# Moving the block sums of a seven-product down-projection in SBUF, and ordering its products by operand

## The chip, the cores and the metric

The kernel runs on one core of a Trainium2 chip. The metric is the device time of one execution in microseconds. Times are medians over several runs; the profile is of one further execution.

## What is computed

The reference is a decoder trunk with 256 tokens (S), width 1024 (D_MODEL) and two layers, in float32. Layer 0 mixes tokens by dilated attention, layer 1 by forgetting attention; behind each stands a SwiGLU feed-forward of inner width 2816 (D_FF). The change touches the feed-forward alone:

```python
def swiglu(h, w_gu, w_down):
    gu = h @ w_gu
    g, u = gu[..., :D_FF], gu[..., D_FF:]
    return (jax.nn.silu(g) * u) @ w_down
```

## The kernel before, in words

**Split products.** Every large operand is kept as a pair of tiles: a high part (ScalarE, L80) and a low part, the rest (VectorE, L84). The names end in `h` and `l`: `wh`, `wl` for weights, `ah`, `al` for activations, `sh`, `sl` and `th`, `tl` for the sums below. A product of two such pairs is three matmuls, high by high (L239), then stationary high by moving low and stationary low by moving high (L244). This is `mm3`; its second argument is the stationary operand, its third the moving one. In the trace, the moving operand comes first: `ps_tr<-th,sh` has `th` moving and `sh` stationary.

**The feed-forward** (`ffn`, from L741). The 22 feature tiles f are worked in order. `up(f)` multiplies the normed activations `xt` (moving) by a tile of gate and up weights (stationary), 48 matmuls of 128x256, forms silu(g)·u, and splits it into half of an activation tile `a`. Two feature tiles make one step j of the down-projection (11 steps). After the up-projection of an even f, the step j = f/2 − 1 is done: `down(j, 0)` and `down(j, 1)` are the first 512 output columns for the two token halves (128x512 matmuls, `a` stationary, the weights moving), and for j < LATE = 9 `down_7(j)` does the other 512 columns for both halves. For these, two token halves, two feature tiles and two column blocks of 256 form a 2x2 block product, which `down_7` does with seven products in place of eight, as Strassen's scheme does. Steps 9 and 10 do it with plain `down` products.

**The seven products.** They are named by their sums: p1, p6, c11, c12, c21, q5, q7; each is 3 matmuls of 128x256, so a call is 21 matmuls, and there are 9 calls a layer. p1 and c11 multiply plain activations `a` by plain weights `w`; c21 multiplies `a` by a block sum of weights, `t`; c12 and q5 multiply a block sum of activations, `s`, by `w`; p6 and q7 multiply `s` by `t`. `combine` (L752) makes `s` on VectorE and allocates it under the tag "v" (7 buffers); `sums_of` (L119) makes `t` and allocates it under the tag "bias" (4 buffers). The accumulators stand in four PSUM tiles: c11 and c12 in one of `acc[0]` (`ps_sc` in the trace), c21 in one of `acc[1]` (`ps_o`), p1 with p6 and q5 with q7 in two more (`ps_tr`). They accumulate over the nine calls; `gather` (L777) then adds p1, p6, q5 and q7 into the residual rows, for token half 0 right after the last call, in a chain of steps on ScalarE (L786) and VectorE (L787 to L795). `residual` (L693) adds the remaining sums.

**What orders the work.** The program is written in the order in which TensorE takes it; the other engines' instructions are placed by a scheduler, with `first()` raising the urgency of some. Weights are loaded on SP's queue and split ahead by `weights`, which runs two tiles ahead of the use; their tiles `wh` and `wl` are rings of four.

**Addresses.** Tiles of one partition row are laid out one behind the other, so the size of a tile sets the address of all that is allocated behind it. In the program before, the starts modulo 128 bytes are: `wh` and `wl` 96, `xt` 32, `ah` and `al` 96, `sh` and `sl` 96, `th` and `tl` 0.

Of the kernel before, what the change touches and what calls it, by code (L numbers as in the profile page):

```python
# [11 lines left out]
F32R = mybir.dt.float32r  # L12
# [5 lines left out]
P = 128  # L18
D = 1024
S = 256  # L20
# [12 lines left out]
def trunk(ctx: ExitStack, tc: tile.TileContext, T, out):  # L33
# [4 lines left out]
    ap = ctx.enter_context(tc.tile_pool(name="ap", bufs=1))  # L38
# [5 lines left out]
    def first():  # L44

        return tc.high_priority(offset=300)

    def psum(tag):
        return ps.tile([P, 512], F32, tag=tag, name=f"ps_{tag}", bufs=2)
# [26 lines left out]
    def split(pair, view, src, early=True, after=None, hold=None):  # L76
        hi, lo = pair
        with first() if early else nullcontext():
            with behind_(hold):
                a = nc.scalar.activation(view(hi), src, AF.Copy)  # L80

            def low(after=None):
                with tc.issue_after(after.ins) if after else nullcontext():
                    return nc.vector.tensor_tensor(view(lo), src, view(hi).bitcast(F32), op=ALU.subtract)  # L84

            if isinstance(after, list):
                return after.append(low)
            return a, low(after)
# [30 lines left out]
    def sums_of(key, w):  # L119

        if key[1] == LATE - 1:
            raw = [wp.tile([P, 1024], F32, tag="raw", name="raw", bufs=5) for _ in range(2)]
        else:
            both_f = ap.tile([P, KT * S], F32, tag=("oth", "otl")[key[1] % 2], name="rawd", bufs=1)
            raw = [both_f[:, c * 1024:(c + 1) * 1024] for c in range(2)]
        for c in range(2):
            nc.sync.dma_start(raw[c], T[key[0]][key[1]][:, c * 1024:(c + 1) * 1024])
        b11, b12, b21, b22 = (raw[f][:, c:c + S] for f in range(2) for c in (512, 768))
        sums = ap.tile([P, 768], F32, tag="pt", name="ts", bufs=3)
        t3, t2, t4 = (sums[:, i * S:(i + 1) * S] for i in range(3))  # L130
        pair = tuple(ap.tile([P, 768], F32R, tag="bias", name=f"t{y}", bufs=4) for y in "hl")
        summed[key] = pair

        def plus(o, a, b):
            nc.vector.tensor_tensor(o, a, b, op=ALU.add)

        def cut(c, after=None, hold=None):
            if c == 0:
                plus(t3, b12, b22)
                plus(b12, b11, b12)  # L140
                plus(t2, b22, b12)
                plus(t4, t2, b21)
            elif c == 2:
                return split(pair, lambda y: y, sums, False, after, hold)
            return split(w, lambda y: y[:, c * 1024:(c + 1) * 1024], raw[c], False, after, hold)

        return [lambda after=None, hold=None, c=c: cut(c, after, hold) for c in range(3)]
# [25 lines left out]
    LATE = NJ - 2  # L173
# [14 lines left out]
    def weights(nm, i, after=None, ahead=AHEAD, hold=None):  # L188

        upto = order.index((nm, i)) + ahead  # L190
        while state["next"] <= min(upto, len(order) - 1):
            key = order[state["next"]]
            cuts = []
            ready[key] = piece(key, cuts)
            for cut in cuts:
                late = key[0][:2] == "dn" and key[1] == LATE - 1
                done = cut(after, state["cut"] if late else hold)
                state["cut"] = done and done[0]
            state["next"] += 1
        return ready.pop((nm, i))  # L200
# [35 lines left out]
    def mm3(o, stat, mov, start, stop, narrow=False):  # L236

        (sh, sl), (mh, ml) = stat, mov
        nc.tensor.matmul(o, sh, mh, start=start, stop=False)  # L239
        n = o.shape[-1]  # L240
        for s, m, end in ((sh, ml, False), (sl, mh, stop)):
            for c in range(0, n, n // 2 if narrow else n):
                u = slice(c, c + (n // 2 if narrow else n))
                last = nc.tensor.matmul(o[:, u], s, m[:, u], start=False, stop=end and u.stop == n)  # L244
        return last

    def both(pair, *idx):
        return tuple(x[idx] for x in pair)
# [108 lines left out]
    o = psum("o")  # L357
# [48 lines left out]
    def square(i):  # L406
        return nc.scalar.activation(part[i].rearrange("p (j s) -> p j s", s=S), xs[i], AF.Square, scale=D ** -0.5)
# [5 lines left out]
    for k in range(KT):  # L413
        if k % 4 == 0:
            w = tuple(wp.tile([P, 2048], F32R, tag=y, name=y, bufs=4) for y in ("wh", "wl"))
        g, u = g_a[:, k:k + 1], slice(k % 4 * 512, k % 4 * 512 + 512)
        with first(), in_order(cut):
            if k == 0:
                a = nc.vector.tensor_scalar(hi[:, k], xk[k], g, None, op0=ALU.mult)
            else:  # L420
                a = nc.scalar.activation(hi[:, k], xk[k], AF.Copy, scale=g)
# [4 lines left out]
        if k in (1, 5, 7):  # L426
            with first(), in_order(cut):
                a = [square(i) for i in {1: (0, 1), 5: (2,), 7: (3,)}[k]][-1]
# [12 lines left out]
    with first(), in_order(cut):  # L441
        a = square(4)
# [22 lines left out]
    x = []  # L465
# [133 lines left out]
    for i, (hq, g, w) in enumerate(a_units):  # L599
        quad = quads[hq]  # L600
        if i == 3:
            o = o_next
# [3 lines left out]
        if i != 3 and (w < 2 or g == 0 and hq > 1):  # L606
            o = psum("mm")
# [7 lines left out]
        if i in (24, 31):  # L615
            x.append(hrow("x"))
            t = len(x) - 1
            nc.sync.dma_start(x[t], T["x"][t * P:(t + 1) * P, :])
        if w < 2:
# [26 lines left out]
            if w == 1:  # L646

                j = i + (hq == 0)
# [92 lines left out]
    def ffn(l, hs, xt, grow, mid):  # L741
# [3 lines left out]
        combos = {}  # L745
# [6 lines left out]
        def combine(j, a):  # L752

            y = ap.tile([P, 512], F32, tag="pt", name="sa4", bufs=3)
            b = a.rearrange("p (b c) -> p b c", c=P)
            z = y.rearrange("p (b c) -> p b c", c=P)
            with first():
                nc.vector.tensor_tensor(z[:, :2], b[:, 1:2].to_broadcast([P, 2, P]), b[:, 0:4:3], op=ALU.subtract)
                nc.vector.tensor_tensor(z[:, 2], z[:, 1], b[:, 0], op=ALU.subtract)
                nc.vector.tensor_tensor(z[:, 3], b[:, 2], z[:, 2], op=ALU.add)  # L760
            combos[j] = tuple(ap.tile([P, 512], F32R, tag="v", name=f"s{x}", bufs=7) for x in "hl")
            split(combos[j], lambda y: y, y)

        def down_7(j):

            if j == 0:
                acc["x"] = [psum("tr") for _ in range(2)]
            c11, c12, c21, _, p1, p6, q5, q7 = (x[:, i * S:(i + 1) * S]
                                                for x in (acc[0][1], acc[1][1], *acc["x"]) for i in range(2))
            a, w, s, t = acts[j], dn[j], combos[j], summed[f"dn{l}", j]  # L770
            for o, (st, i), (mv, c) in ((p1, (a, 0), (w, 512)), (p6, (s, 2), (t, S)), (c11, (a, 2), (w, D + 512)),
                                        (c12, (s, 3), (w, D + 768)), (c21, (a, 3), (t, 512)), (q5, (s, 1), (w, 768)),
                                        (q7, (s, 0), (t, 0))):
                mm3(o, both(st, ALL, slice(i * P, (i + 1) * P)), both(mv, ALL, slice(c, c + S)),
                    j == 0 and any(o is y for y in (p1, c11, c21, q5)), j == LATE - 1 and any(o is y for y in (p6, q7)))

        def gather(t):  # L777

# [23 lines left out]
        def gated(g, u, shape):  # L802
            sa = ap.tile([P, 512], F32, tag="qr", name="sa", bufs=3)
            sg, a = (sa[:, i * S:(i + 1) * S].rearrange("p (a b) -> p a b", a=shape) for i in range(2))
            with first():
                nc.scalar.activation(sg, g, AF.Silu)
                nc.vector.tensor_tensor(a, u, sg, op=ALU.mult)
            return a
# [51 lines left out]
        pair = [psum(("o", "mm")[l]) for _ in range(2)]  # L860
# [9 lines left out]
        wt, o = weights(f"gu{l}", 2), psum(("mm", "o")[l])  # L870
# [10 lines left out]
        split(acts[0], lambda y: y, tr)  # L881
        nc.scalar.activation(pair_of(0), tr, AF.Copy)
        combine(0, rows_f.pop(0))
        third = act(2)
        up(3)
        gu = o.rearrange("p (a c b) -> p a c b", a=2, c=2)
        a = gated(gu[:, :, 0, :], gu[:, :, 1, :], 2)
# [6 lines left out]
        for f in range(2, NF):  # L894
            if f > 3:
                up(f)
            if f % 2 == 0:
                j = f // 2 - 1
                dn[j] = weights(f"dn{l}", j)
                down(j, 0, narrow=j >= LATE)  # L900
                if j < LATE - 1:
                    down(j, 1)
                    down_7(j)
        dn[NJ - 1] = weights(f"dn{l}", NJ - 1)
        down(LATE - 1, 1)
        down_7(LATE - 1)
        gather(0)
        last = down(NJ - 1, 0, (0, 1))
# [168 lines left out]
    for i, (hq, w) in enumerate(b_units):  # L1077
# [4 lines left out]
        o = psum("mm")  # L1082
        if w < 2:
# [15 lines left out]
            if w == 1:  # L1099
                j = i + 1  # L1100
# [39 lines left out]
    for o, (a, b) in zip(acc, ((0, 512), (512, 256), (768, 256))):  # L1140
        s = slice(a, a + b)
# [8 lines left out]
    v = ap.tile([P, 2], F32, tag="rs", name="rs", bufs=4)  # L1150
# [10 lines left out]
    for n in range(2):  # L1161
        s = slice(n * 256, n * 256 + 256)
# [3 lines left out]
        s = slice(n * 256, 256 + n * 352)  # L1166
# [88 lines left out]
```

## Time and profile before

| | us |
|---|---|
| median of 3 runs | 732.58 (732.35 to 734.78) |
| profiled execution, own time | 732.42 |
| its span in the profile | 730.6 |
| TensorE busy | 722.6 (99%) |
| VectorE busy | 566.9 (78%) |
| ScalarE busy | 416.9 (57%) |
| mean granted clock of TensorE | 0.997 |

In the profile, PE is TensorE's matmul and PEld its weight load, DVE is VectorE, ACT ScalarE, POOL GpSimd, SP SyncE; L239 is line 239 of the kernel. A group's row ends with its busy time and the mean duration of one in ns, or gives min/median/max. Matmuls are pipelined, so that the durations of successive ones overlap: a 128x256 matmul lasts some 280 ns in the profile while the next starts 113 to 120 ns after it. What a stretch of matmuls costs is read from start times, not from durations. A row of the timeline has the start in us, the duration in us, the engine and the instruction, and in brackets the idle time before it and what ended that. A row of the table of windows has the window, its length, and each engine's busy time in it with the instructions that touch it.

### The profile page before, as it was taken

What the parts mean: (1) busy time and instruction counts of PE and PEld (TensorE: products, weight loads), DVE (VectorE), ACT (ScalarE), POOL (GpSimd) and SP (SyncE); (2) the same over time, 40 slices, a digit from 0 to 9 for tenths busy, and PEclk for the clock granted to TensorE, in tenths of its full rate; (3) what the DMA queues carried; (4) which work ended last, traced back from release to release, by engine and by line L of the source; (5) the groups of instructions that cost most, each with busy time, mean ns of one, the idle gap of its engine ahead of it and who ended that gap; (6) DMA issues with size and microseconds to landing.
All of it is one profiled execution on the core that took longest, in us unless ns stands there. A gap on an engine that the chain in (4) does not pass through costs nothing.

```text
span 730.6 us, 14753 instructions
## 1 busy us (share of the span) xinstructions
PE 722.6 (99%) x5988; PEld 674.5 (92%) x5988; DVE 566.9 (78%) x938; ACT 416.9 (57%) x659; POOL 83.5 (11%) x118
## 2 busy tenths in 40 slices
PE   9999999999999999999999999999999999999996
PEld 7999989999988899999999989999889999999995
DVE  6997998998996788877778484586878977777825
ACT  7646747648545656655546353587475655545621
POOL 0600206008105000000000014120010000000001
PEclk9999999999999999999999999999999999999998
DMA  9865856855864494766348442883548576534601
GB/s 335 309 203 174 225 180 187 278 198 146 269 196 159 124 334 163 255 209 210 121 130 266 141 156 88 297 267 130 172 148 342 175 239 213 182 127 146 219 1 59
DMA packets 55045, 141.97 MB, mean 194 GB/s; under 512 B 20257, under 2 KB 21441, under 8 KB 54977
## 3 DMA queue, kind: packets, MB, share of 16 engines
q1 hardware_dynamic: 54832, 140.81, 59.0%
q8 instruction: 47, 0.77, 0.4%
q10 hardware_dynamic: 144, 0.21, 0.1%
q14 instruction: 22, 0.17, 0.1%
HBM read 136.00 MB, written 1.07 MB: 188 GB/s over the span
## 4 chain that ended last, share of the span: by engine, by line
PE 96%; ACT 1%; DMA 1%; DVE 1%; issue 0%; SPq 0%; POOL 0%; POOLq 0%; DVEq 0%; ACTq 0%
PE ps_mm L244 44%; PE ps_mm L239 22%; PE ps_sc L244 7%; PE ps_o L244 6%; PE ps_sc L239 4%; PE ps_o L239 3%; PE ps_tr L244 2%; PE ps_o L350 2%; PE ps_tr L239 1%; DMA otl<-in_lead 1%; PE ps_sc L513 1%; PE ps_tr L232 1%; PE ps_tr L338 1%; PE ps_sc L1006 0%; PE ps_sc L495 0%; ACT wh L80 0%
## 5 line engine op out<-in xcount | busy, mean ns | idle before, releaser
L239 PE MATMUL ps_mm<-xt,wh 128*128 128x256 f32 x1120 | 311.5, 278 | 0.1
L244 PE MATMUL ps_mm<-xt,wl 128*128 128x256 f32 x1120 | 309.9, 277 | 0.1
L244 PE MATMUL ps_mm<-xt,wh 128*128 128x256 f32 x1120 | 309.7, 277 | 0.0
L80 ACT ACTIVATE wh<-raw 128x1024 fp32r<-128x1024 f32 x204 | 210.4, 1056 | 136.9 <-PE ps_mm L244 71.4
L84 DVE TENSOR_TENSOR wl<-raw,wh 128x1024 fp32r<-128x1024 f32 x204 | 248.5, 1242 | 28.6 <-ACT wh L80 28.6
L239 PEld LDWEIGHTS ps_mm<-xt,wh 128*128 128x128 f32 x1120 | 210.3, 188 | 3.2 <-issue 1.7
L244 PEld LDWEIGHTS ps_mm<-xt,wl 128*128 128x128 f32 x1120 | 210.6, 188 | 0.3 <-DVE wl L84 0.3
L244 PEld LDWEIGHTS ps_mm<-xt,wh 128*128 128x128 f32 x1120 | 210.4, 188 | 0.2
L824 DVE TENSOR_TENSOR a<-ps_mm,sa 128x256 f32<-128x256 f32 x38 | 16.0, 422 | 50.4 <-PE ps_mm L244 50.4
L209 POOL TENSOR_SCALAR rs<-ssq 128x1 f32<-128x1 f32 x7 | 2.7, 391 | 419.6 <-ACT junk L218 419.6
L80 ACT ACTIVATE wh<-rawd 128x1024 fp32r<-128x1024 f32 x32 | 33.6, 1056 | 28.5 <-PE ps_mm L244 22.6
L239 PE MATMUL ps_mm<-wh,xt 128*128 128x512 f32 (+1 forms) x144 | 49.8, 346 | 0.0
L244 PE MATMUL ps_mm<-wh,xt 128*128 128x512 f32 (+1 forms) x149 | 49.2, 335 | 0.0
L244 PE MATMUL ps_mm<-wl,xt 128*128 128x512 f32 (+1 forms) x149 | 49.1, 335 | 0.0
L322 POOL COPY v<-v 32x256 f32<-32x256 f32 x64 | 40.4, 631 | 69.4 <-ACT v L317 66.8
L84 DVE TENSOR_TENSOR wl<-rawd,wh 128x1024 fp32r<-128x1024 f32 x32 | 39.0, 1225 | 1.7 <-ACT wh L80 1.6
L244 PEld LDWEIGHTS ps_mm<-wl,xt 128*128 128x128 f32 x149 | 28.0, 188 | 3.1
L244 PEld LDWEIGHTS ps_mm<-wh,xt 128*128 128x128 f32 x149 | 27.6, 188 | 3.3 <-DVE xt L84 0.3
L239 PEld LDWEIGHTS ps_mm<-wh,xt 128*128 128x128 f32 x144 | 27.0, 188 | 3.5 <-issue 0.3
L569 ACT COPY pt<-turned 128x1280 uint16<-128x1280 uint16 x12 | 19.4, 1671 | 13.9 <-DMA turned<-pt 13.9
L821 ACT ACTIVATE sa<-ps_mm 128x256 f32<-128x256 f32 x38 | 14.6, 383 | 21.2 <-PE ps_mm L244 20.6
L566 POOL COPY pt<-p 128x1280 uint16<-128x1280 uint16 x12 | 16.6, 1404 | 79.8 <-DVE p L546 38.8
(297 smaller groups left out, 1207.7 us busy)
## 6 DMA issues: line engine op xcount, KB each, us to landing
raw<-in_gu SPq DMA_DIRECT2D x88, 512.0 KB, 5.0
raw<-in_a_in SPq DMA_DIRECT2D x68, 512.0 KB, 4.9
rawd<-in_dn SPq DMA_DIRECT2D x32, 512.0 KB, 4.8
raw<-in_b_in SPq DMA_DIRECT2D x24, 512.0 KB, 4.7
raw<-in_dn SPq DMA_DIRECT2D x12, 512.0 KB, 4.8
raw<-in_a_out SPq DMA_DIRECT2D x8, 512.0 KB, 5.2
raw<-in_b_out SPq DMA_DIRECT2D x8, 512.0 KB, 4.0
bias<-sums SPq DMA_DIRECT2D x8, 384.0 KB, 5.7
```

What stands on the lines that cost most here:

```text
L80: a = nc.scalar.activation(view(hi), src, AF.Copy)
L84: return nc.vector.tensor_tensor(view(lo), src, view(hi).bitcast(F32), op=ALU.subtract)
L232: nc.tensor.transpose(tr[:, k * P:(k + 1) * P], xn[:, kk * P:(kk + 1) * P], ident)
L239: nc.tensor.matmul(o, sh, mh, start=start, stop=False)
L244: last = nc.tensor.matmul(o[:, u], s, m[:, u], start=False, stop=end and u.stop == n)
L322: nc.gpsimd.tensor_copy(v[1 + a % 2][n:n + 32, a // 2 * S:a // 2 * S + S], by_t[a * 32:a * 32 + 32, t, g])
L338: nc.tensor.transpose(tr[:, i * P:(i + 1) * P], b, ident)
L350: nc.tensor.matmul(o[h * HD:(h + 1) * HD], v[:, c:c + HD], w(h), start=start, stop=stop)
L566: nc.gpsimd.tensor_copy(split16.rearrange("p (t c) -> p t c", t=2), parts(quad["pt"][pr, h]))
L569: nc.scalar.copy(parts(w), turned.rearrange("p (t c) -> p t c", t=2))
L821: nc.scalar.activation(sg, g, AF.Silu)
L824: nc.vector.tensor_tensor(a, u, sg, op=ALU.mult)
```

## The change

First, the tiles of `s` and of `t` are allocated larger and used from an offset: `t` begins 96 bytes into its slot (24 elements), `s` 64 bytes (16 elements). A slot of `t` grows from 3072 to 3200 bytes, one of `s` from 2048 to 2176. So `s` comes to lie at 32 modulo 128 and `t` at 96, while all that is allocated behind moves by a multiple of 128 bytes (`a` by 896) and keeps its place modulo 128. Second, the order of the seven products changes from p1, p6, c11, c12, c21, q5, q7 to q5, p6, q7, c12, c21, p1, c11; the flags that open and close an accumulation move to the first and last product of each PSUM tile.

```diff
-        pair = tuple(ap.tile([P, 768], F32R, tag="bias", name=f"t{y}", bufs=4) for y in "hl")
+        pair = tuple(ap.tile([P, 800], F32R, tag="bias", name=f"t{y}", bufs=4)[:, 24:792] for y in "hl")
...
-            combos[j] = tuple(ap.tile([P, 512], F32R, tag="v", name=f"s{x}", bufs=7) for x in "hl")
+            combos[j] = tuple(ap.tile([P, 544], F32R, tag="v", name=f"s{x}", bufs=7)[:, 16:528] for x in "hl")
...
-            for o, (st, i), (mv, c) in ((p1, (a, 0), (w, 512)), (p6, (s, 2), (t, S)), (c11, (a, 2), (w, D + 512)),
-                                        (c12, (s, 3), (w, D + 768)), (c21, (a, 3), (t, 512)), (q5, (s, 1), (w, 768)),
-                                        (q7, (s, 0), (t, 0))):
+            for o, (st, i), (mv, c) in ((q5, (s, 1), (w, 768)), (p6, (s, 2), (t, S)), (q7, (s, 0), (t, 0)),
+                                        (c12, (s, 3), (w, D + 768)), (c21, (a, 3), (t, 512)), (p1, (a, 0), (w, 512)),
+                                        (c11, (a, 2), (w, D + 512))):
                 mm3(o, both(st, ALL, slice(i * P, (i + 1) * P)), both(mv, ALL, slice(c, c + S)),
-                    j == 0 and any(o is y for y in (p1, c11, c21, q5)), j == LATE - 1 and any(o is y for y in (p6, q7)))
+                    j == 0 and any(o is y for y in (q5, p6, c12, c21)), j == LATE - 1 and any(o is y for y in (p1, q7)))
```

On TensorE, the end of a call of `down_7` in layer 0 and the first matmuls of the up-projection behind it (`ps_mm<-xt,wh`) stand as follows; the rows with a minus are before, those with a plus after.

```order
 L244 MATMUL ps_o<-th,al 128x256
-L239 MATMUL ps_tr<-wh,sh 128x256
-L244 MATMUL ps_tr<-wl,sh 128x256
-L244 MATMUL ps_tr<-wh,sl 128x256
-L239 MATMUL ps_tr<-th,sh 128x256
-L244 MATMUL ps_tr<-tl,sh 128x256
-L244 MATMUL ps_tr<-th,sl 128x256
+L239 MATMUL ps_tr<-wh,ah 128x256
+L244 MATMUL ps_tr<-wl,ah 128x256
+L244 MATMUL ps_tr<-wh,al 128x256
+L239 MATMUL ps_sc<-wh,ah 128x256
+L244 MATMUL ps_sc<-wl,ah 128x256
```

Products q5 and q7, with `s`, have left the end of the call, and p1 and c11, with `a`, stand there; a last row of c11 follows, and then the up-projection as before. In place of p1, a call begins with q5 behind the 512-wide matmuls of `down(j, 1)`. No matmul is added or dropped.

On VectorE, the steps of `gather` in layer 1 and the residual sum behind them stand as follows.

```order
 L790 TENSOR_TENSOR h_b_out_6538<-h_b_out_6538,u 128x256
 L792 TENSOR_TENSOR u<-u,ps_tr 128x256
+L693 TENSOR_TENSOR hf_8640<-ps_sc,h_b_out_6538 128x512 x2
 L793 TENSOR_TENSOR u<-u,ps_tr 128x256
-L693 TENSOR_TENSOR hf_8640<-ps_sc,h_b_out_6538 128x512 x2
 L795 TENSOR_TENSOR h_b_out_6618<-h_b_out_6618,u 128x512
```

The residual of token half 0 now comes ahead of the last step that prepares token half 1 (L793); layer 0 has the same. GpSimd keeps its order. In one place of layer 1, ScalarE and VectorE split `t` ahead of one weight tile that it followed before, and SP's queue has one `rawd` load (weights for `t`) ahead of a `raw` load (up weights).

## The prediction, made before the changed kernel ran

> **What bounds the kernel now.** I read the page's busy shares first, then the chain that ended last, then the waits of TensorE alone.
>
> ```profile
> span 730.6 us, 14753 instructions
> PE 722.6 (99%) x5988; PEld 674.5 (92%) x5988; DVE 566.9 (78%) x938; ACT 416.9 (57%) x659; POOL 83.5 (11%) x118
> PE 96%; ACT 1%; DMA 1%; DVE 1%; issue 0%; SPq 0%; POOL 0%; POOLq 0%; DVEq 0%; ACTq 0%
> PE ps_o L359 <- DVE mhalf L66: 0.9, 1, 0.9
> ```
>
> TensorE (PE) is busy for 99% of the span, the chain is PE for 96%, and the only time that PE waits for another engine is 0.9 us at the very start. So the time is the sum of the spacings between successive matmuls, and an edit that adds or removes no matmul moves the time only by changing that spacing or by opening a wait. Next I read the matmuls by tile and shape, since the change moves 128x256 matmuls only.
>
> ```profile
> L244 PE MATMUL ps_mm<-xt,wl 128*128 128x256 f32 x1120 | 309.9, 277 | 0.1
> L239 PE MATMUL ps_tr<-th,sh x36: 284/284/287, 279.3 to 714.8; 128*128 128x256 f32 x36
> L244 PE MATMUL ps_tr<-tl,sh x36: 280/280/281, 279.4 to 715.0; 128*128 128x256 f32 x36
> L244 PE MATMUL ps_sc<-wh,sl x16: 280/283/283, 280.2 to 678.0; 128*128 128x256 f32 x16
> ```
>
> In a row, moving operand and then stationary operand stand behind the arrow; three numbers are min/median/max in ns. All four rows are the same shape and type, and yet `xt` against `w` takes 277 ns, while the products of `down_7` take 280 to 284. The difference has no releaser; it belongs to the operands. These durations overlap, so the spacing must come from start times: windows whose ends are the starts of PE stretches give it.
>
> ```profile
> core 0: us, PE busy (x) PEld busy (x) DVE busy (x) ACT busy (x) POOL busy (x), PEclk, DMA share, GB/s
> 281.39:286.83 5.44, 5.44 (x50) 5.44 (x49) 5.44 (x8) 5.44 (x8) 0.00 (x0) 1.00 0.47 135
> 305.71:308.21 2.50, 2.50 (x23) 2.50 (x21) 2.10 (x3) 0.77 (x2) 0.00 (x0) 1.00 0.27 92
> 308.21:319.10 10.89, 10.89 (x98) 10.89 (x97) 7.50 (x12) 5.51 (x8) 0.00 (x0) 1.00 0.66 214
> 401.11:410.06 8.95, 8.95 (x77) 8.90 (x75) 5.05 (x7) 3.95 (x7) 0.00 (x0) 1.00 0.46 156
> 691.45:700.40 8.95, 8.95 (x77) 8.90 (x75) 5.05 (x7) 3.95 (x7) 0.00 (x0) 1.00 0.01 2
> ```
>
> The second row is one `down_7`: 21 matmuls in 2.50 us, 119.0 ns each (x23 counts two that were still in flight). The first and third are the up-projections that follow a `down_7`: 48 and 96 matmuls in 5.44 and 10.89 us, 113.4 ns each. The last two are up-projections too, of the same tiles, but they follow 512-wide matmuls directly: 76 in 8.95 us, 117.8 ns each. The granted clock is 1.00 in every row and DMA share runs from 0.01 to 0.66 without a pattern, so neither explains it. So one and the same stream has two steady spacings, 113.4 and 117.8, and what stands ahead of it decides which. Once entered, it keeps it for the whole stretch. That is the lever, and the danger, of this change: it alters both addresses and what stands ahead.
>
> **The change, part by part.** Inside one `down_7` I read the start of each product (three matmuls) in the timeline.
>
> ```profile
> 305.71 0.28 PE L239 MATMUL ps_tr<-wh,ah 128*128 128x256 f32 x1
> 306.06 0.28 PE L239 MATMUL ps_tr<-th,sh 128*128 128x256 f32 x1
> 306.42 0.28 PE L239 MATMUL ps_sc<-wh,ah 128*128 128x256 f32 x1
> 306.77 0.28 PE L239 MATMUL ps_sc<-wh,sh 128*128 128x256 f32 x1
> 307.13 0.28 PE L239 MATMUL ps_o<-th,ah 128*128 128x256 f32 x1
> 307.49 0.28 PE L239 MATMUL ps_tr<-wh,sh 128*128 128x256 f32 x1
> 307.85 0.28 PE L239 MATMUL ps_tr<-th,sh 128*128 128x256 f32 x1
> 308.21 0.28 PE L239 MATMUL ps_mm<-xt,wh 128*128 128x256 f32 x1
> ```
>
> *Products with block sums s.* p6, c12, q5 and q7 take 0.36 us each (the steps from 306.06, 306.77, 307.49 and 307.85), 1.44 us of the call. After the change their stationary lies at 32 modulo 128 and their moving operand at 96 (w and t both): the two operands stand 64 bytes apart, as they do in the up-projection, where the moving one is at 32 and the stationary one at 96. Before, s and w both lay at 96. No row shows these tiles so placed, so I take the two steady spacings of the up-projection as bounds: 12 x 113.4 = 1.361 us, or 12 x 117.8 = 1.414 us. The gain is 0.026 to 0.079 us a call, and with 18 calls (x36 above, two such products a call) 0.47 to 1.4 us. For the value I take the slower end: after the change the first of them follows 512-wide matmuls directly, and the two stretches above that did so fell at 117.8. That is −0.5 us. Below nothing I set no bound here, since the present 120 ns is the slowest steady spacing that these rows show.
>
> *Products with plain activations a.* p1 and c11 take 0.35 us each, c21 0.36: 1.06 us. a and w keep their addresses modulo 128, both at 96; t moves from 0 to 96, so all three products now have both operands at 96, nine in a row. The nearest such run is a stretch of 128x256 `down` products:
>
> ```profile
> 719.43 0.28 PE L244 MATMUL ps_o<-wl,ah 128*128 128x256 f32 x1
> 719.55 0.28 PE L244 MATMUL ps_o<-wh,al 128*128 128x256 f32 x1
> 719.67 0.28 PE L239 MATMUL ps_o<-wh,ah 128*128 128x256 f32 x1
> ```
>
> Its spacing is 0.12 us, and 9 x 0.12 = 1.08: a loss of 0.02 us a call, +0.36 us over 18. The bounds are 0 (they stay at 1.06) and this.
>
> The Trainium skill bears on both terms. In "TensorE: Matmul & The Clock Gate", Part 2, step ①, it says of the two SBUF read ports that "Loading the next tile's weights doesn't steal SBUF read bandwidth from the running matmul." By that the place of s and t would be worth nothing, and these two terms would sum to zero; the equal shapes at 277 and 284 ns above speak against it, though they do not show that the port is the reason.
>
> *The up-projections behind it.* Of the 18 calls, 16 are followed by one (the x16 of the row with `wh,sl`): 2 with 48 matmuls and 14 with 96, 1440 matmuls in all. They now follow a product of w with a (both at 96) instead of one of t with s (0 and 96). Both leave 119 to 120 ns behind them. I expect the stream to be caught at 113.4 again, cost 0. If it falls to 117.8, each matmul costs 4.4 ns more; that is a rival below.
>
> *Moved starts and stops.* The flags are attributes of the matmuls: nothing is added.
>
> *Order of q5 first.* It needs s at the first matmul instead of the fourth, 0.35 us earlier. s is written ahead: its low half at 275.2 the first time, done 0.69 us later, and the first product with s starts at 279.3 (the row of `th,sh`), so 3.4 us are in hand; cost 0, and without them 0.35 us a call.
>
> ```profile
> L84 DVE TENSOR_TENSOR sl<-sa,sh x18: 684/687/693, 275.2 to 688.8; 128x512 fp32r<-128x512 f32 x18
> 582.31 1.06 ACT L80 ACTIVATE wh<-raw 128x1024 fp32r<-128x1024 f32 x1 [1.77 <-PE ps_tr L244]
> 585.41 1.22 DVE L84 TENSOR_TENSOR wl<-raw,wh 128x1024 fp32r<-128x1024 f32 x1
> ```
>
> *Slot of w.* Now c11 is the last to read it, where it was q5, so the slot is freed one product, 0.36 us, later. ScalarE waits there, as at 582.31, and behind it on its queue stand the next splits; DVE's second half then starts at 585.41. The slot is one of a ring of four and holds up weights that are used only behind the next `down_7`, so not before the up-projections that begin at 582.4 are through, 10.89 us later at 593.3; the split ends at 586.6, and these 6.7 us cover it: cost 0, and without cover at most 16 x 0.36 = 5.8 us. The same reserve covers the one place in layer 1 where the split of the sums comes ahead of a weight split (0.83 us by th's instruction at most) and where a pair of `rawd` loads goes ahead of one `raw` load on SP's queue.
>
> *Gather.* p1 ends sixth instead of first, so the first step of `gather(0)` starts later.
>
> ```profile
> 713.62 0.39 ACT L786 ACTIVATE u<-ps_tr 128x256 f32<-128x256 f32 x1 [3.28 <-PE ps_tr L244]
> 715.09 0.28 PE L244 MATMUL ps_tr<-th,sl 128*128 128x256 f32 x1
> 715.41 0.42 DVE L789 TENSOR_TENSOR u<-ps_tr,u 128x256 f32<-128x256 f32 x1 [0.61 <-PE ps_tr L244]
> 717.48 1.37 DVE L693 TENSOR_TENSOR hf<-ps_sc,h_b_out 128x512 f32<-128x512 f32 x2 [0.41 <-PE ps_sc L244]
> ```
>
> ScalarE's copy at 713.62 waited for the p1 and p6 tile; p1's last matmul will now start some 0.36 us ahead of 715.09 and end 0.28 later, so the copy starts near 715.0, 1.4 us later. L789 has 0.61 us idle ahead of it now, and L693 0.41 us; L793, of 0.4 us, moves behind L693. I sum 0.61 + 0.41 + 0.4 = 1.4 us against 1.4 us: the residual starts where it did or within 0.1 us of it, in both layers. PE has `down` products of the other half queued and waits for nothing there. Cost 0; without that cover, 0.1 us each.
>
> **Sum.** Profiled execution 732.42 us, 1.8 us above its span of 730.6, and 0.16 us under the median of 732.58 us; the terms are differences, so I put them on the median: −0.5 + 0.36 = −0.1 at the slow end of s, −1.4 + 0.36 = −1.0 at the fast end. Transitions fall from six between a and s products to one; each cost the 3 to 4 ns by which p6 or c21 exceed their kind, so 18 x 5 x 0.003 = 0.3 us at best. I take half of the way, 0.4 us of gain: **732.2 us**, with an own range of 730.9 to 733.0.
>
> **Rivals.**
>
> *Slower: the up-projections are caught at 117.8.* Place: the first matmuls behind each of 16 calls. Price: 1440 x 4.4 ns = 6.3 us, so 732.2 + 6.3 = **738.5 us**. It decides at the last product of `down_7`: the stretches at 401.11 and 691.45 show that the same operands fall there if what stands ahead is wrong, and after the change the nine matmuls ahead have their operands at 96 as those 512-wide ones have. For 113.4 speaks that all 16 such blocks now, which follow 128x256 matmuls at 119 to 120 ns, are caught there, and that spacing is kept. It is all or nothing, as the 16 places are alike. Chance 0.21.
>
> *Faster: s products at 113.4 and more.* −1.0 as above; if the 152 matmuls at 401.11 and 691.45 were caught at 113.4 too, 152 x 4.4 ns = 0.67 us more, and transitions 0.3: −2.0, **730.6 us**. That is still within the bound. To pass it, the 512-wide products must move as well, which keep address and order. Chance of over 0.3% (2.2 us): 0.10, as the tiles of a move by 896 bytes, an odd multiple of 128, and I can't exclude that some larger period counts.
>
> *Placement is worth nothing* (the change is made, but the durations are set by something else, such as which tile is read twice): **732.6 us**. Within the forecast's range; I give it 0.12. It is the time by the skill's sentence on the ports as well.
>
> **How the numbers follow.** A difference of 0.3%, 2.2 us, is about what a measurement of this kernel can tell from none. Forecast with its range and the null: 0.57 + 0.12 = 0.69 within; slower 0.21, all from the up-projections; faster 0.10. Since the slower case holds just over 2 in 10, the range reaches to it: from 730.4, the faster rival with 0.2 spare, to 738.8, its 738.5 with 0.3 spare.
>
> **What would show it.** In the profile of the changed kernel: the groups of `ps_tr<-wh,sh` and `ps_tr<-th,sh` at 277 to 281 ns and not 280 to 284; `down_7` at 2.43 to 2.49 us between its first start and the next stretch; the a products at 0.36 us each; the blocks behind it at 10.89 us (right) or 11.31 (96 x 117.8, the slower rival); PE's waits still one of 0.9 us; L693 of gather within 0.1 us of where PE's `ps_sc` ends. Wrong would be a time under 730.4, a PE wait at a `down_7`, or blocks of 10.89 us together with a time over 733.

## The result, and the profile after

The changed kernel takes 737.26 us (median of 5 runs, 737.02 to 737.93), against 732.58 before; the ratio is 1.0059 with a 95% interval of 1.0048 to 1.0070. The median is 4.7 us longer, where 0.4 us of gain had been forecast. The profiled execution took 737.26 us, 4.84 us more than the one before.

The page after has the same bound, and the waits of TensorE are the same single one:

```profile
span 735.5 us, 14753 instructions
PE 727.4 (99%) x5988; PEld 678.3 (92%) x5988; DVE 566.8 (77%) x938; ACT 415.3 (56%) x659; POOL 82.5 (11%) x118
PE ps_o L359 <- DVE mhalf L66: 0.9, 1, 0.9
```

PE's busy time grew by 4.8 us with the same 5988 matmuls and no new wait. All of the loss is spacing. Summed over the trace from start to start, three kinds of matmul make it: those of `xt` against `w` +4.27 us, the 512-wide products with `a` +0.87, all others −0.3 together.

The windows of a `down_7` and of the up-projections behind four of them (columns as in the prediction) show the first part:

```profile
308.12:310.60 2.48, 2.48 (x22) 2.48 (x21) 2.06 (x3) 0.62 (x1) 0.00 (x0) 1.00 0.14 45
310.60:321.50 10.90, 10.90 (x98) 10.90 (x97) 7.49 (x12) 5.62 (x8) 0.00 (x0) 1.00 0.65 215
326.77:338.08 11.31, 11.31 (x98) 11.31 (x97) 7.68 (x13) 5.62 (x8) 0.00 (x0) 1.00 0.66 212
618.96:630.27 11.31, 11.31 (x99) 11.31 (x97) 7.68 (x13) 5.62 (x8) 0.00 (x0) 1.00 0.66 212
667.82:678.72 10.90, 10.90 (x98) 10.90 (x97) 5.87 (x10) 5.62 (x8) 0.00 (x0) 1.00 0.30 98
```

Of the sixteen blocks behind `down_7`, four (from 326.77, 343.36, 602.37 and 618.96) last 11.31 us, 117.8 ns a matmul; the other twelve stay at 113.5. That is 4 x 0.41 = 1.64 us. Clock and DMA share of a slow and a fast block are alike (1.00; 0.66 and 0.65).

The larger part lies where the diff has no line: in layer 0's dilated mixer, which runs ahead of the first `down_7` (that one starts at 278.9 us before the change). These are two of its long stretches of `xt` against `w`, 240 matmuls each, before and then after.

```profile
114.54:141.84 27.30, 27.30 (x242) 27.17 (x241) 24.81 (x40) 22.42 (x34) 10.23 (x16) 1.00 0.79 232
169.36:196.66 27.30, 27.30 (x242) 27.17 (x241) 24.21 (x30) 17.03 (x16) 14.87 (x19) 1.00 0.76 219
```
```profile
114.46:142.82 28.36, 28.36 (x242) 28.23 (x240) 25.21 (x40) 22.60 (x36) 10.71 (x16) 1.00 0.76 234
170.33:198.69 28.36, 28.36 (x242) 28.23 (x241) 24.93 (x30) 17.91 (x17) 13.89 (x19) 1.00 0.78 227
```

Each lost 1.06 us. The timeline at the entry of the first, before and after, with two matmuls in a row where it says x2:

```profile
114.06 0.40 PE L244 MATMUL ps_mm<-wl,xt 128*128 128x256 f32 x2
114.30 0.40 PE L244 MATMUL ps_mm<-wh,xt 128*128 128x256 f32 x2
114.54 0.28 PE L239 MATMUL ps_mm<-xt,wh 128*128 128x256 f32 x1
```
```profile
114.01 0.39 PE L244 MATMUL ps_mm<-wl,xt 128*128 128x256 f32 x2
114.24 0.39 PE L244 MATMUL ps_mm<-wh,xt 128*128 128x256 f32 x2
114.46 0.28 PE L239 MATMUL ps_mm<-xt,wh 128*128 128x256 f32 x1
```

The four matmuls ahead take 0.48 us before and 0.45 after: they came some 118 ns apart and now come 113 apart, and the stretch behind them does the opposite. So slow neighbours don't make a slow stretch. The operands are the same, at the same addresses (`xt` and `w` lie ahead of the slots of `s` and didn't move), but the stretch was entered otherwise.

Third, the 512-wide products with `a`, one of their groups, before and after:

```profile
L239 PE MATMUL ps_o<-wh,ah 128*128 128x512 f32 x44 | 17.2, 392 | 0.0
```
```profile
L239 PE MATMUL ps_o<-wh,ah 128*128 128x512 f32 x44 | 17.4, 396 | 0.0
```

Same instructions, same place modulo 128, 4 ns more each in mean duration; from start to start it is 228.5 ns before and 231.7 after. What changed is `a`'s place modulo 256: 96 before, 224 after, since the larger slots of `s` push it by 896 bytes, seven times 128.

### The profile page after: what moved, and what is told of

It is laid out like the page before. It is cut to its first block, busy times and chain, and to the rows that moved or that the text cites. A ratio compares the mean times of both kernels' runs of the same rounds, so it can differ in the third digit from the quotient of the medians.

```text
span 735.5 us, 14753 instructions
## 1 busy us (share of the span) xinstructions
PE 727.4 (99%) x5988; PEld 678.3 (92%) x5988; DVE 566.8 (77%) x938; ACT 415.3 (56%) x659; POOL 82.5 (11%) x118
## 3 DMA queue, kind: packets, MB, share of 16 engines
HBM read 136.00 MB, written 1.07 MB: 186 GB/s over the span
## 4 chain that ended last, share of the span: by engine, by line
PE 95%; DVE 1%; ACT 1%; DMA 1%; issue 0%; SPq 0%; POOL 0%; POOLq 0%; DVEq 0%; ACTq 0%
PE ps_mm L244 44%; PE ps_mm L239 22%; PE ps_sc L244 7%; PE ps_o L244 6%; PE ps_sc L239 3%; PE ps_o L239 3%; PE ps_tr L244 2%; PE ps_o L350 2%; PE ps_tr L239 1%; DMA otl<-in_lead 1%; PE ps_sc L513 1%; PE ps_tr L232 1%; PE ps_tr L338 1%; PE ps_sc L1006 0%; PE ps_sc L495 0%
```

## The experiments

All compare with the kernel before on the same chip. The parts of the change were first taken apart: order of the products, places of s and t modulo 128, and the shift of what lies behind the slots of `s`.

**Order alone.** The order and the flags of the change, the tiles of before.

```diff
-            for o, (st, i), (mv, c) in ((p1, (a, 0), (w, 512)), (p6, (s, 2), (t, S)), ...
+            for o, (st, i), (mv, c) in ((q5, (s, 1), (w, 768)), (p6, (s, 2), (t, S)), ...
```

> New order of the seven products, every tile where it was before. If the order alone makes the loss (theory A: what stands ahead of the up-projections sends them to 117.8 ns): four or more of the sixteen up-projection blocks behind down_7 last 11.2 us instead of 10.8, 512-wide products with a stay at 228.5 ns, time 734 to 737 us. If the 128-byte shift of the tiles behind v makes it (theory B): all sixteen blocks at 10.8 us, time 732.3 to 733.0. If the places of s and t make it (theory C): also 732.3 to 733.0, with down_7 at 2.50 us.

Measured 733.67 us against 733.16, ratio 1.0003 (0.9994 to 1.0012). All sixteen blocks kept 113.5 to 113.7 ns a matmul. Order alone costs nothing that the measurement can tell, so theory A falls as a cause by itself.

**Shift alone.**

```diff
+ap.tile([P, 32], F32, tag="pad", bufs=1)   # 128 bytes, ahead of qr, fm, a
```

> Order and places of s and t as before; only an unused tile of 128 bytes behind the tiles of v, so that a, fm, qr and all behind lie 128 bytes further. Theory B (the shift alone): 512-wide products with a go from 228.5 to 232 ns (+0.9 us), the two 240-matmul stretches of the dilated mixer may fall to 117.8 ns (+2.1 us), time 733.5 to 737. Theory A and theory C: no change, 732.3 to 733.0.

Measured 734.47 us, 1.0013 (1.0004 to 1.0021). The 512-wide products with `a` went up by 0.98 us, and in the profile the mixer's stretches fell to 117.8 ns; none of the sixteen blocks behind `down_7` did, one of which is the second row:

```profile
114.35:142.71 28.36, 28.36 (x242) 28.23 (x240) 25.24 (x41) 22.79 (x36) 10.71 (x16) 1.00 0.77 234
326.47:337.37 10.90, 10.90 (x98) 10.90 (x97) 7.50 (x12) 5.52 (x8) 0.00 (x0) 1.00 0.66 210
```

The two losses make 3.1 us in the profiled execution, which was the longest of its eleven (735.45; the shortest 733.36), but the median rose by 1.3 us only. So the mixer's 2.1 us can't have been in most of the executions; this is worked out from the times, not seen.

**Places of s and t alone.** Old order; the two lines of the tiles; 128 unused bytes bring `a` and `fm` back modulo 256 (with two buffers of the tiny tile `rs` for room).

```diff
+... tag="bias", name=f"t{y}", bufs=4)[:, 24:792]
+... tag="v", name=f"s{x}", bufs=7)[:, 16:528]
+ap.tile([P, 32], F32, tag="pad", bufs=1)   # ahead of qr, fm, a
-    v = ap.tile([P, 2], F32, tag="rs", name="rs", bufs=4)
+    v = ap.tile([P, 2], F32, tag="rs", name="rs", bufs=2)
```

> Old order; s and t at their new places; an unused tile of 128 bytes and two rather than four buffers of the tiny tile rs bring a, fm, qr back to their place modulo 256. Theory C (places of s and t alone): down_7 longer or the up-projections behind it at 117.8 ns, time 734 to 737. Theory A and B: 732.0 to 733.0, the four products with s a little faster at most.

Measured 733.22 us, 1.0001 (0.9991 to 1.0011). `down_7` gained 0.46 us over the 18 calls (44.50 us against 44.96), and two of the sixteen blocks fell (at 372.25 and 647.00), which costs 0.8. The first of them, and the one behind it, which did not fall:

```profile
372.25:383.56 11.31, 11.31 (x98) 11.31 (x97) 7.68 (x13) 5.70 (x9) 0.00 (x0) 1.00 0.36 121
388.81:399.70 10.89, 10.89 (x98) 10.89 (x97) 8.45 (x12) 5.51 (x8) 0.00 (x0) 1.00 0.87 279
```

**The whole change without the shift.** Against the changed kernel:

```diff
+ap.tile([P, 32], F32, tag="pad", bufs=1)   # ahead of qr, fm, a; rs with 2 buffers
```

> The whole change, with the same unused tile and two buffers of rs, so that a, fm, qr lie where they did modulo 256. Theory B: the loss goes, 732.0 to 733.0, 512-wide products with a at 228.5 ns. Theory A: up-projection blocks at 11.2 us stay, 734 to 737. Theory C: as e3, 734 to 737.

Measured 733.60 us, 1.0006 (0.9997 to 1.0016). No block fell, neither did the mixer's stretches, and the 512-wide products with `a` were back at 228.4 ns. Its first long stretch of the mixer, and a block behind `down_7`:

```profile
114.73:142.03 27.30, 27.30 (x242) 27.18 (x240) 24.44 (x38) 21.55 (x31) 10.21 (x16) 1.00 0.82 224
324.86:335.76 10.90, 10.90 (x98) 10.90 (x97) 7.50 (x12) 5.62 (x8) 0.00 (x0) 1.00 0.64 212
```

Moving the tiles behind by 128 bytes undoes the loss, so the shift of theory B is needed for it, and A and C have no net loss without it. But the shift alone had cost 1.3 us, not 4.7, so the parts don't add. (The two buffers of `rs` went with the 128 bytes and were not tried alone.) The next runs fill in the pairs: the changed kernel once more; its order with the 128 unused bytes, without the two lines of the tiles; and these two lines alone.

> The changed kernel unaltered, as the measure of the next three on their chip: 736.5 to 738 us, four up-projection blocks at 11.2 us, 512-wide products with a at 232 to 233 ns.

Measured 737.44 us (before on this chip 732.64), 1.0063 (1.0051 to 1.0075), with the same four blocks slow as in the first profile, and the mixer's two stretches.

> New order and 128 bytes more behind v, s and t at their old places modulo 128. If the loss is a joint effect of order and shift (theory A with B): 736 to 738 us, up-projection blocks at 11.2 us. If the three parts only add (+0.2 for the order and +0.95 for the shift were measured): 734.2 to 734.6 us.

Measured 736.05 us, 1.0048 (1.0036 to 1.0060): the joint effect that theory A with B asked for in time, but not at its place. No block behind `down_7` fell; the mixer's two stretches did, the 512-wide products with `a` lost 0.96, and in that execution TensorE waited 0.9 us near 263 us for VectorE's split of `xt`.

```profile
114.19:142.55 28.36, 28.36 (x243) 28.23 (x241) 25.09 (x40) 22.66 (x35) 10.67 (x16) 1.00 0.77 233
327.54:338.44 10.90, 10.90 (x98) 10.90 (x97) 7.50 (x12) 5.62 (x8) 0.00 (x0) 1.00 0.65 210
```

> Old order; s and t at their new places, and with them the 896 bytes by which everything behind moves. If the loss is a joint effect of places and shift (theory C with B): 736 to 738 us. If the parts only add: 734.0 to 734.4 us.

Measured 738.09 us, 1.0076 (1.0064 to 1.0088), the slowest of all. Five blocks of 96 fell, and one of 48. Three of the sixteen, the middle one undisturbed:

```profile
310.40:321.70 11.30, 11.30 (x98) 11.30 (x97) 7.67 (x13) 5.51 (x8) 0.00 (x0) 1.00 0.65 208
326.97:337.87 10.90, 10.90 (x99) 10.90 (x97) 7.50 (x12) 5.51 (x8) 0.00 (x0) 1.00 0.64 212
651.35:662.65 11.30, 11.30 (x98) 11.30 (x97) 7.67 (x13) 5.51 (x8) 0.00 (x0) 1.00 0.39 121
```

So blocks behind `down_7` fall only where s and t have their new places: in the old order two of them without the shift, and five and a half with it; in the new order none and four.

Which blocks these are can be read from the programs. The larger slots are odd multiples of 128 bytes, so in a call `sh` and `sl` start at 32 or 160 modulo 256, and `th` and `tl` at 96 or 224. In the changed kernel the four blocks that fell stand behind the four calls with `sh` at 160, `sl` at 32, `th` at 96 and `tl` at 224, and none of the other twelve calls has these four places; the same holds in its second profile. With the old order and the shift, the six that fell are all four calls with 32, 160, 224 and 96 and both with 160, 160, 224 and 96; without the shift they are both calls with 160, 160, 96 and 224. In these four profiles the places of `sh`, `sl`, `th` and `tl` modulo 256 tell all 64 blocks without an exception. Which places are the bad ones depends on the order and on the shift, and no run moved one of the four alone.

**Only `a` put back.** Against the changed kernel:

```diff
+ap.tile([P, 32], F32, tag="pad", bufs=1)   # behind qr and fm, ahead of a; rs with 2 buffers
```

> The changed kernel, with an unused tile of 128 bytes only ahead of the activations a (two buffers of rs), so that a, t and the tiles behind return to their place modulo 256, while qr, fm and qk's partners stay shifted. If the place of a is what sends the up-projections behind down_7 to 117.8 ns: blocks at 10.8 us, 512-wide products at 228.5 to 229 ns, time 733.5 to 735.5, with the stretches of the dilated mixer still slow in the profile. If fm's place matters for them too: 737.

Measured 735.34 us, 1.0036 (1.0023 to 1.0048). No block behind `down_7` ran at 117.8 ns; the last one lost 1.09 us around one wait of TensorE for ScalarE, not to its spacing. So for these blocks to fall in the new order, the place of `a`, or of the tiles behind it that moved with it, counts too. The mixer's two stretches, with `fm` still shifted, stayed slow at 28.36 us each. The group of 512-wide products shown above is back at 392 ns:

```profile
L239 PE MATMUL ps_o<-wh,ah 128*128 128x512 f32 x44 | 17.3, 392 | 0.0
```

**Only `a` shifted, only `fm` shifted, 256 bytes instead of 128, and only `t` at its new place**, each on the kernel before.

```diff
+ap.tile([P, 32], F32, tag="pad", bufs=1)   # ahead of a
...
+ap.tile([P, 32], F32, tag="pad", bufs=1)   # ahead of qr, fm
+ap.tile([P, 32], F32, tag="pad2", bufs=1)  # ahead of a
...
+ap.tile([P, 64], F32, tag="pad", bufs=1)   # ahead of qr, fm, a
...
+... tag="bias", name=f"t{y}", bufs=4)[:, 24:792]
```

> The kernel before with an unused tile of 128 bytes ahead of a only: a, and the tiles behind it, are shifted, fm and qr are not. If a's place alone slows the 512-wide products: 512-wide products with a at 232 ns (+0.9 us), the mixer's two long stretches as before, time +0.8 to +1.1 us. If any displacement of any tile sends stretches astray: +2 us or more.

Measured 733.85 us, 1.0015 (1.0006 to 1.0024): the 512-wide products with `a` +0.96 us (228.5 to 232.0 ns), the mixer's two stretches as before.

```profile
L239 PE MATMUL ps_o<-wh,ah 128*128 128x512 f32 x44 | 17.4, 395 | 0.0
```

> The kernel before with 128 bytes ahead of qr and fm and another 128 ahead of a: qr and fm are shifted, a and all behind lie 256 bytes further. If the place of fm sends the mixer's two stretches of 240 to 117.8 ns: both last 28.15 us, 512-wide products stay at 228.5 ns, profile +2.1 us, time +0.3 to +2.1 us. If a does it: no change.

Measured 735.06 us, 1.0029 (1.0018 to 1.0040). The 512-wide products stayed at 228.5 ns, and yet the median rose by 2.1 us. The profiled execution was the shortest of twelve (732.95; the others 734.00 to 736.89) and shows both stretches undisturbed, so this profile can't say where the 2.1 us lay.

> The kernel before with 256 bytes, not 128, ahead of qr, fm, a and all behind. If it is the place modulo 256 that counts: no change in any stretch, time within 0.3 us of before. If any displacement counts: as the shift by 128, +1 us or more.

Measured 733.12 us against 732.94, 0.9998 (0.9989 to 1.0007). No stretch of `xt` against `w` with 48 matmuls or more changed, and neither did the 512-wide products:

```profile
114.80:142.10 27.30, 27.30 (x242) 27.18 (x240) 24.37 (x38) 21.85 (x32) 10.23 (x16) 1.00 0.81 234
L239 PE MATMUL ps_o<-wh,ah 128*128 128x512 f32 x44 | 17.3, 392 | 0.0
```

So 128 bytes count and 256 don't: it is the place modulo 256 that matters here, not that a tile was moved at all.

> The kernel before with t alone at its new place (96 bytes further; its larger slots lie behind a and shift nothing by an odd 128). If the new place of t makes its products faster and flips no up-projection: down_7 2.47 to 2.49 us, time -0.2 to -0.4 us. If it sends up-projections behind down_7 to 117.8 ns: +0.4 us for each, 733.5 or more.

Measured 732.83 us, 0.9998 (0.9989 to 1.0007). `down_7` gained 0.29 us over 18 calls, no block behind it fell, and the time doesn't show it; in the profiled execution, the longest of its eleven at 734.04 us, another stretch of the mixer, the 222 matmuls that start at 25.5 us, ran at 117.8 ns. So a stretch can fall without `fm`'s shift too.

**Two more profiles of `fm` shifted alone, and s or t alone with order and shift.** The last two take the change without the line of `t`, and without the line of `s` but with the 128 unused bytes.

> The kernel with qr and fm alone shifted, profiled a second time. If the place of fm sends the mixer's two stretches of 240 to 117.8 ns in most executions: both last 28.15 us and the time is 734.5 to 736. If the 2.1 us by which its median was longer lie elsewhere: both last 27.10 us in a run of 734 or more.

> The same kernel as e13, profiled a third time: 28.15 us for both stretches in a run of 734.5 to 736 if the place of fm does it, 27.10 us in a run of 734 or more if the loss lies elsewhere.

One execution of each, 734.33 and 733.65 us; the first of the mixer's two stretches in the one and in the other:

```profile
113.96:142.32 28.36, 28.36 (x243) 28.23 (x241) 25.05 (x40) 22.67 (x35) 10.30 (x16) 1.00 0.78 231
```
```profile
114.64:141.95 27.31, 27.31 (x243) 27.18 (x241) 24.45 (x39) 22.05 (x33) 10.23 (x16) 1.00 0.79 228
```

The same program does both. The place of `fm` seems to make the fall possible: of eleven profiles with `fm` shifted, seven show both stretches slow and four neither; of the seven with `fm` at its old place or 256 bytes further, before among them, none does. The chip may have a part in it: on one chip all four profiles with `fm` shifted are slow, on another one of four, and neither chip has a profile with `fm` at its old place.

The traces show where the two outcomes part. Ahead of the first stretch stand 512-wide matmuls, and ahead of those the scores (`ps_sc<-fm,fm`), the matmuls that read `fm`. In the seven slow profiles the second of these 512-wide matmuls is followed after 235 ns and the third after 229 or 230; in none of the eleven others do the two steps come so. So the stretch inherits its spacing from an entry 5.3 us ahead, right behind the scores, which fits `fm`'s place as a cause without showing it. What decides in a single execution isn't settled.

> The changed kernel with t back at its old place (slots of 3072 bytes); s at its new one, a shifted. If the place of s sends the up-projections astray: blocks of 11.2 us behind down_7, 736.5 to 738. If that of t: all at 10.8 us, 735.5 to 736.5, as order and shift without places (736.05).

> New order, t at its new place, s at its old one modulo 128, a and fm shifted by 128 bytes. If the place of t sends the up-projections astray: blocks of 11.2 us, 736.5 to 738. If that of s: all at 10.8 us, 735.5 to 736.5.

Measured 734.37 us, 1.0016 (1.0007 to 1.0026), and 733.93 us, 1.0006 (0.9997 to 1.0016). No block behind `down_7` fell in either; the fourth one, which fell with both places, here with s alone and then with t alone:

```profile
324.40:335.30 10.90, 10.90 (x99) 10.90 (x97) 7.49 (x12) 5.62 (x8) 0.00 (x0) 1.00 0.63 210
```
```profile
325.82:336.72 10.90, 10.90 (x98) 10.90 (x97) 7.50 (x12) 5.62 (x8) 0.00 (x0) 1.00 0.65 210
```

In the new order and with the shift, neither place alone made them fall, in one profile each; both together did, in two. Both were quicker than I expected for either theory, since the mixer's stretches stayed at 27.3 us in their profiles; the 512-wide loss of 0.9 us is in both.

No version beats the kernel before by more than the measurement can tell.

## Why the prediction was wrong, point by point

**The outcome.** I forecast 732.2 us, a small gain, and got 737.26, a loss. The time lies close to the slower rival's 738.5, but that is chance: of the 4.84 us in the profile, the rival's place, the blocks behind `down_7`, gave 1.64, and the rest came from matmuls for which I had no term.

**The bound** was right: PE's spacing is the time, and no wait came up.

**The products with s and with a.** I put the change of `down_7` at −0.1 to −1.0 us, and another −0.3 for transitions. The starts of the seven products after:

```profile
308.12 0.28 PE L239 MATMUL ps_tr<-wh,sh 128*128 128x256 f32 x1
308.47 0.28 PE L239 MATMUL ps_tr<-th,sh 128*128 128x256 f32 x1
308.82 0.28 PE L239 MATMUL ps_tr<-th,sh 128*128 128x256 f32 x1
309.17 0.28 PE L239 MATMUL ps_sc<-wh,sh 128*128 128x256 f32 x1
309.53 0.28 PE L239 MATMUL ps_o<-th,ah 128*128 128x256 f32 x1
309.88 0.28 PE L239 MATMUL ps_tr<-wh,ah 128*128 128x256 f32 x1
310.25 0.28 PE L239 MATMUL ps_sc<-wh,ah 128*128 128x256 f32 x1
310.60 0.28 PE L239 MATMUL ps_mm<-xt,wh 128*128 128x256 f32 x1
```

The four products with s take 1.41 us, as at the slow end (1.414); the three with a 1.07. Over the 18 calls the s products went from 25.78 to 25.63 us (−0.15, against −0.5), the a products from 19.18 to 19.25 (+0.07, against +0.36), and `down_7` from 44.96 to 44.88: −0.08. The −0.15 holds 0.22 us lost at one place that I had not seen: in the first call of layer 0, the new order comes out with the first matmuls of p6 and q7 next to each other, and each of the two is followed only 0.22 to 0.23 us later; every kernel with the new order has it. So the slow end was right as a spacing, and both terms were too large because I took them from starts rounded to 0.01 us: a call's s products took 1.432 us before, not 1.44, and its a products 1.07 after, not 1.08. That the two errors nearly cancel is luck. Nothing is left for the 0.3 us of transitions, which I had also miscounted: before, there are five in a call, not six.

**The up-projections behind.** "I expect the stream to be caught at 113.4 again, cost 0" failed in four blocks of sixteen: 1.64 us. The mechanism of the slower rival is what happened, 6.3 us was its price for all sixteen, and "all or nothing, as the 16 places are alike" was the false step in it: the places are not alike, since the slots of s and t now start alternately at two places modulo 256, and these places tell which block falls. "Once entered, it keeps it for the whole stretch" was read too far as well: in every profile the first 76 matmuls of the stretch that starts at 401.11 before, and of its twin in layer 1, come 117.8 ns apart, but the 44 behind them, entered anew after a step of 0.34 us, came at 113.3 in 29 cases and at 117.8 in 7.

**"a and w keep their addresses modulo 128"**: true, and the wrong measure. This is the step that failed most. I read the two classes off tiles whose places I compared modulo 128 alone, and took 128 for the period. I did name a larger period, and counted it for the faster side only. The 512-wide products "keep address and order", I wrote; their `a` moved by 896 bytes and cost 0.87 us. And I put nothing down for what lies outside the feed-forward, without a reason, while the diff's tile sizes moved `fm` too: 2.1 us of the 4.84 in the mixer. 1.64 + 2.1 + 0.87 are 4.6 us; the rest is in short stretches and small groups (a stretch of 120 at 458.63, in layer 1's mixer, lost 0.50, and one of 72 behind it gained 0.31). These two go with the shift of `a` and the tiles behind it: the stretch of 120 runs at 117.8 ns in all eight profiles with `a` shifted by 128 bytes and at 113.3 in the ten others.

The Trainium skill's sentence in "TensorE: Matmul & The Clock Gate", Part 2, step ①, that loading weights doesn't steal read bandwidth from the running matmul, does not cover this: with `a` and the tiles behind it moved by 128 bytes the 512-wide matmuls on `a` lost 3.5 ns each (228.5 to 232.0). The runs don't show by which path.

**Order of q5, slot of w, scheduling elsewhere**: no wait of PE in the changed kernel, so cost 0 as I said. **Gather**: right.

```profile
719.79 0.39 ACT L786 ACTIVATE u<-ps_tr 128x256 f32<-128x256 f32 x1 [4.75 <-PE ps_tr L244]
719.94 0.40 PE L239 MATMUL ps_sc<-wh,ah 128*128 128x512 f32 x1
722.32 1.31 DVE L693 TENSOR_TENSOR hf<-ps_sc,h_b_out 128x512 f32<-128x512 f32 x2
```

The copy starts 0.15 us ahead of `down_7`'s end at 719.94, and the residual 2.38 us behind it, where it was 2.27 before (715.21 to 717.48): 0.1 us late, and PE doesn't wait.

## What to carry to other kernels

Where TensorE never waits, a change of a tile's size is a change of every address behind it: list what moves, modulo 256 and not only modulo 128, and look at all matmuls on those tiles, also in stages that the diff doesn't touch. A stream of short matmuls can have two steady spacings, and its gain elsewhere is small against losing one long stretch to the slower; compare the windows of every long stretch before and after, in more than one execution. When moving a tile, pad its neighbours so that they stay where they were, and measure that version beside the other.

## What the runs showed of the hardware that was not expected

- 512-wide matmuls of weights against `a`, with the moving operand at 96 modulo 256, came 228.4 to 228.7 ns apart in the ten profiles with the stationary operand at 96, and 231.5 to 232.1 in the eight with it at 224 (means of 267 steps). 128 bytes of padding switch between the two, 256 bytes change nothing.
- The 128x256 stream of `xt` against `w` has two steady spacings, 113.3 and 117.8 ns, at the same granted clock. It keeps the one with which it starts for up to 240 matmuls, and can change it where a longer step breaks the stretch.
- Behind `down_7`, the places modulo 256 of the call's four block-sum tiles told which of the two came, block by block. In the mixer the same program took either in different executions, and what tells those entries apart stays open.
- Executions of one kernel can differ by it: with `fm` shifted alone, twelve ran from 732.95 to 736.89 us, and three profiles of this kernel show it with and without the 2.1 us.
